# Expert weights loaded as halves of one matrix in 16 KB runs, and x1 stored in natural order, partly from ACT's queue

## The chip, the cores and the metric

The kernel runs on one core of one Trainium2 chip. The metric is the device time of one execution in microseconds. The kernel before took 1311.16 us, the median of three runs (1309.23 to 1311.32). Engines are named as in the profile: PE is TensorE (PEld its weight loads), DVE is VectorE, ACT is ScalarE, POOL is GpSimd, SP is SyncE, which here issues nearly all loads and stores. A name with a q behind it (SPq) is that engine's sequencer.

## What is computed

One decoder layer on 512 tokens of 1024 features, all in float32. A mixer (a causal convolution group and a dilated attention group) gives z = alpha * x + mix, and a layer norm of z gives x1. A router picks 4 of 32 experts for each token, and each expert is a SwiGLU block:

```python
g = jnp.minimum(xb @ w_gate[e] + b_gate[e], 7.0)
u = jnp.clip(xb @ w_up[e] + b_up[e], -7.0, 7.0)
hdn = (u + 1.0) * g * jax.nn.sigmoid(1.702 * g)
y = hdn @ w_down[e] + b_down[e]
```

The gated sum of the chosen experts' y is added to alpha * x1, and a second layer norm gives the output. Each expert has three matrices of 1024 x 1024 float32, 4 MB each, so 12 MB per expert and 403 MB in all, and every weight is read once.

## The kernel before, in words

**Front (0 to about 270 us).** The mixer, the first layer norm, the router and the ranks of tokens within their experts. The order of this part is made by a planner (class Plan): each operation is entered with its engine, an estimated duration, what it reads and writes, and a group; a list scheduler places the operations by rank (the longest chain behind an operation, less a tuned offset for its group, LAGS), and every engine's program, and the order in which DMAs are issued, follows the planned order. DMAs are one planned resource, D, and all of them are issued by SP (`dma`, line 409). At its end, x1 of each of the four token tiles is made in `acc` (lines 911 to 923: scale on ACT, times g, plus b, each in two halves on DVE or POOL) and stored to the DRAM scratch `x1d` (line 926), one 512 KB store per tile. The features of a token stand in `acc` in a permuted order: 1024 = 8 blocks of 4 quarters of 32 columns, with quarter outermost. So a row of `x1d` (4 rows of 256 per token) is one quarter. ACT's later work at that place is a copy for the last router logits, a table load, and the exp of the gates (line 1255).

**Experts (about 270 to 1260 us).** Experts are taken in an order by size: each expert has room for 32, 64, 96 or 128 tokens, that is 1 to 4 "rows" (78 rows in all: five experts of four rows, eight of three, fifteen of two, four of one). A row is 32 tokens, whose four quarters stand on the four groups of 32 partitions. Four rows make a group, 20 in all. `gather` (line 1008) fetches the rows of a group from `x1d` by indirect DMAs from POOL, `xpose` (line 1049) transposes 32 x 32 blocks on DVE, so that features stand on partitions; both run ahead of the expert that needs them (LOOK = 2: rows are gathered during an expert, and transposed, at the earliest, at the end of the next).

`expert` (line 1066) runs one expert in six steps, one per weight piece of 2 MB. There are seven places for pieces in SBUF (six `wt`, one `wb`); `advance` (line 319) issues the loads of later pieces as places come free. A gate/up piece (line 297) holds 256 input rows of both matrices, so it takes two loads; a down piece (line 306) holds 512 rows of w_down. A partition gets single matrix rows, 4 KB in one run:

```python
SP.dma_start(t[:, :, gu], src[0, ei, c * 256:(c + 1) * 256, :].rearrange("e (k p) f -> p (e k) f", p=128))
```

In the steps c = 0 to 3 each row of the expert runs 2 x 4 matmuls of 32 stationary columns and 512 moving ones (gate and up side by side, one per quarter of the outputs; line 1078). A float32 matmul is two records in the trace, so a row has 64 records of 107 ns each in this phase, spread over four column groups of TensorE. Gate and up of a row share one PSUM bank (`ps[i]`: 2 x 256). After c = 3 `swiglu` (line 1055) runs five operations per row on DVE (clamp of gate, clamp of up, two products, and the transpose into `hT`, line 1064) and one on ACT. Then two down pieces follow (lines 1104 and 1107): two neighbouring rows share matmuls of 512 columns, a single row takes 256. The result is copied as a high and a low part (lines 1121 and 1123), and `combine` (line 1125) later adds a group's results to `acc` by one-hot matmuls (lines 1135 and 1136), two pairs at a time between the steps (`tick`, `fill`).

**End.** The bias sum (line 1320), the second layer norm of the four tiles (`outputs`, line 1414), the last expert's row (`last_rows`, line 1449), and a scatter of 32 rows. The norm's g and b are read through views that undo the permuted order.

Of the kernel before, what the change touches and what calls it, by code (L numbers as in the profile page):

```python
# [14 lines left out]
AF = mybir.ActivationFunctionType  # L15
# [249 lines left out]
def tile_layer(ctx: ExitStack, tc: tile.TileContext, x, positions, w_in, conv_w, conv_b, conv_ln_g,  # L265
# [143 lines left out]
    def dma(nbytes, dst, src, r=(), w=(), **kw):  # L409
        return op("D", max(0.45, nbytes / 359e3), lambda e: SP.dma_start(dst() if callable(dst) else dst, src), r, w, **kw)  # L410
# [465 lines left out]
    stores = []  # L876
# [4 lines left out]
    for tt in range(TT):  # L881
# [12 lines left out]
        def choose(e, lst=lst, lg=lg, tt=tt):  # L894
# [17 lines left out]
        zv, gv, bv = ((lambda f=f: f().rearrange("p (b q c) -> p q b c", b=8, q=4)) for f in (  # L912
            lambda zn=zn: zn.t(), lnps[0], lnps[1]))
        az = acc[:, tt].rearrange("p (q b c) -> p q b c", b=8, q=4)
# [3 lines left out]
        for hf in range(2):  # L918
            bs = slice(hf * 4, hf * 4 + 4)
            op("VG", (0.6, 1.25), (lambda az, zv, gv, bs: lambda e: (V if e == "V" else G).tensor_tensor(  # L920
                az[:, :, bs], zv()[:, :, bs], gv()[:, :, bs], OP.mult))(az, zv, gv, bs),
               [zn, ("ln", 0)], [("z", tt, 0), ("z", tt, 1), ("x1", tt, hf)])
            op("VG", (0.6, 1.25), (lambda az, bv, bs: lambda e: (V if e == "V" else G).tensor_tensor(
                az[:, :, bs], az[:, :, bs], bv()[:, :, bs], OP.add))(az, bv, bs), [("ln", 1)], [("x1", tt, hf)])
        stores.append(("x1d", tt))
        dma(524288, x1d[tt * 512:(tt + 1) * 512, :].rearrange("(p q) c -> p (q c)", q=4), acc[:, tt], r=[("x1", tt, hf) for hf in range(2)], w=[("x1d", tt)])
# [122 lines left out]
    def xpose(st, rows=None):  # L1049
# [3 lines left out]
        V.transpose(st["xT"][:, n].rearrange("p r b t -> p (r b t)"), st["xg"][:, n].rearrange("p r c -> p (r c)"))  # L1053
# [506 lines left out]
```

## Time and profile before

| | |
|---|---|
| median of three runs | 1311.16 us |
| the profiled execution | 1312.21 us |
| its span in the trace | 1310.2 us |
| mean granted clock of TensorE | 0.977 of full speed |
| PE / PEld / DVE / ACT / POOL busy | 1231.8 / 562.2 / 649.0 / 280.7 / 185.6 us |
| DMA moved | 441.95 MB, of it 436 MB read from DRAM |

Busy time of TensorE is not TensorE at its peak: matmuls are pipelined, four of them run side by side here, and their ends are modelled. Pace is better read from the starts of two groups in a timeline and the number of records between them. Idle time of an engine matters only where something on the path to the end waits for it. [...]

### The profile page before, as it was taken

The numbers are of one execution on the slowest core, as the hardware profiler recorded it, in microseconds if no ns is written. First come the engines' busy times: TensorE is split into PE (matmuls) and PEld (weight loads), VectorE is DVE, ScalarE is ACT, GpSimd is POOL, SyncE is SP. The second block draws the span as 40 slices with busy tenths as digits, with TensorE's granted clock in tenths as the row PEclk, the third lists the DMA queues.
The fourth block names the chain that finished last, engine by engine and source line by source line (L and its number), as shares of the span: only waits on it lengthen the run. The fifth ranks groups of instructions, "written<-read, shape, count | busy, mean of one in ns | idle before, by whom it ended". The sixth has DMA issues, their size and how long they took to land. (4 is left out here: it accounts for less than half of the span.)

```text
span 1310.2 us, 25490 instructions
## 1 busy us (share of the span) xinstructions
PE 1231.8 (94%) x10578; PEld 562.2 (43%) x10578; DVE 649.0 (50%) x1516; ACT 280.7 (21%) x551; POOL 185.6 (14%) x158
## 2 busy tenths in 40 slices
PE   8989999889998999999999999998999998999984
PEld 7867767723232333332333323343345333534342
DVE  5999855745442443343424434353425462444474
ACT  4677782311000000000000001110111110111122
POOL 2854101321011011011010110011100101000003
PEclk9999999889999999999999999999999999999987
DMA  9400335679999999999999999999999999999991
GB/s 286 165 1 1 129 113 141 241 287 389 408 406 406 408 406 406 409 396 406 409 406 408 406 406 405 409 405 408 405 408 408 405 406 406 391 364 356 409 401 71
DMA packets 126003, 441.95 MB, mean 337 GB/s; under 512 B 8279, under 2 KB 16615, under 8 KB 125884
## 3 DMA queue, kind: packets, MB, share of 16 engines
q1 hardware_dynamic: 122092, 429.98, 84.4%
q0 software_dynamic: 3792, 10.29, 2.2%
q8 instruction: 85, 1.39, 0.4%
q14 instruction: 34, 0.28, 0.1%
HBM read 435.99 MB, written 4.33 MB: 336 GB/s over the span
## 5 line engine op out<-in xcount | busy, mean ns | idle before, releaser
L1078 PE MATMUL gd<-wt,xTg 128*32 128x512 f32 x4304 | 494.9, 596 | 9.9 <-DMA wt<-in_exp_w_up_dram 4.9
L1078 PEld LDWEIGHTS gd<-wt,xTg 128*32 128x32 f32 x4304 | 146.3, 110 | 287.4 <-issue 273.8
L1104 PE MATMUL gd<-wt,hT 128*32 128x512 f32 x1472 | 184.7, 594 | 16.2 <-DVE hT L1064 13.2
L1017 POOL DMA_INDIRECT xg<-x1d,idx x78 | 74.7, 957 | 879.5 <-DVE tk L1046 837.0
L1137 DVE TENSOR_TENSOR acc<-acc,cb 128x512 f32<-128x512 f32 x160 | 102.4, 678 | 167.5 <-PE cb L1136 167.4
L1060 ACT ACTIVATE sg<-gm 128x256 f32<-128x256 f32 x78 | 32.5, 417 | 594.9 <-DVE gm L1059 594.9
L1123 DVE TENSOR_TENSOR yl<-gd,wh 32x256 fp32r<-32x256 f32 (+1 forms) x140 | 73.8, 527 | 141.7 <-ACT wh L1121 140.4
L1121 ACT ACTIVATE wh<-gd 32x256 fp32r<-32x256 f32 (+1 forms) x140 | 64.7, 462 | 280.0 <-PE gd L1104 201.3
L1104 PEld LDWEIGHTS gd<-wt,hT 128*32 128x32 f32 x1472 | 54.9, 110 | 126.9 <-issue 83.9
L1059 DVE TENSOR_SCALAR gm<-gd 128x256 f32<-128x256 f32 x77 | 30.9, 401 | 107.9 <-PE gd L1078 107.9
L546 PE MATMUL bk<-wt,wh 128*128 128x512 f32 (+1 forms) x352 | 80.9, 377 | 0.7 <-ACT sg L590 0.7
L1078 PE MATMUL gd<-wb,xTg 128*32 128x512 f32 x624 | 73.5, 593 | 1.3 <-DMA wb<-in_exp_w_up_dram 1.3
L1135 PE MATMUL cb<-wh,cg 128*128 128x512 f32 (+2 forms) x160 | 72.4, 453 | 2.2 <-DVE cg L1129 2.2
L1107 PE MATMUL gd<-wt,hT 128*32 128x256 f32 x1056 | 68.0, 387 | 6.2 <-DMA wt<-in_exp_w_down_dram 4.9
L584 DVE SCALAR_TENSOR_TENSOR bk<-u,cT,bk 128x512 f32<-128x512 f32 x88 | 66.2, 753 | 1.9
L546 PEld LDWEIGHTS bk<-wt,wh 128*128 128x128 f32 x352 | 61.2, 189 | 13.3 <-ACT sg L590 1.1
L1136 PE MATMUL cb<-yl,cg 128*128 128x512 f32 (+2 forms) x160 | 64.4, 402 | 0.0
L1135 PEld LDWEIGHTS cb<-wh,cg 128*128 128x128 f32 (+2 forms) x160 | 30.8, 192 | 57.9 <-issue 40.4
L1107 PEld LDWEIGHTS gd<-wt,hT 128*32 128x32 f32 x1056 | 41.3, 111 | 31.8 <-issue 11.7
L1063 DVE SCALAR_TENSOR_TENSOR um<-um,tk,sg 128x256 f32<-128x256 f32 x78 | 39.7, 509 | 8.9
L546 PE MATMUL bk<-wt,wl 128*128 128x512 f32 (+1 forms) x176 | 41.5, 378 | 1.6 <-DVE wl L537 1.6
L582 POOL TENSOR_TENSOR cv<-cv,acc 128x512 f32<-128x512 f32 x28 | 40.1, 1435 | 8.2 <-ACT acc L579 6.7
(336 smaller groups left out, 1210.3 us busy)
## 6 DMA issues: line engine op xcount, KB each, us to landing
wt<-in_exp_w_gate_dram SPq DMA_DIRECT2D x112, 1024.0 KB, 19.7
wt<-in_exp_w_up_dram SPq DMA_DIRECT2D x112, 1024.0 KB, 18.9
wt<-in_exp_w_down_dram SPq DMA_DIRECT2D x52, 2048.0 KB, 20.4
wb<-in_exp_w_down_dram SPq DMA_DIRECT2D x12, 2048.0 KB, 17.1
wb<-in_exp_w_gate_dram SPq DMA_DIRECT2D x16, 1024.0 KB, 18.4
wb<-in_exp_w_up_dram SPq DMA_DIRECT2D x16, 1024.0 KB, 19.5
wt<-in_w_in_dram SPq DMA_DIRECT2D x3, 2048.0 KB, 13.1
acc<-in_x_dram SPq DMA_DIRECT2D x8, 512.0 KB, 8.0
```

What stands on the lines that cost most here:

```text
L546: P.matmul(b.t[:, ts], w.t[:, k], xx[:, k, ts], start=(pas == 0 and k == 0), stop=(pas == 2 and k == KT - 1))
L582: op("G", 1.25, (lambda t: lambda e: G.tensor_tensor(cv[:, c], cv[:, c], t.t, OP.add))(t), [t], [k])
L584: op("V", 0.663, (lambda j: lambda e: V.scalar_tensor_tensor(b.t, u[:, c, j:j + T], cT[:, c, j:j + 1], b.t, op0=OP.mult, op1=OP.add))(j), ...
L1017: G.indirect_dma_start(out=xg[:, r], out_offset=None, in_=x1d[:, :], in_offset=bass.IndirectOffsetOnAxis(ap=idx[:, r:r + 1], axis=0))
L1078: P.matmul(ps[i][q * 32:(q + 1) * 32], st["xT"][:, r, c * 2 + k], w[:, k, :, :, q], start=False, stop=(c == 3 and k == 1))
L1104: P.matmul(d[j * 32:(j + 1) * 32], st["hT"][:, r + j % 2, c * 4 + k], w[:, k, 2 * (j // 2):2 * (j // 2) + 2], **kw)
L1107: P.matmul(d[j * 32:(j + 1) * 32, 0:256], st["hT"][:, r, c * 4 + k], w[:, k, j], **kw)
L1121: S.activation(st["yh"][o], a, AF.Copy)
L1123: V.tensor_tensor(st["yl"][o], a, st["yh"][o].bitcast(F32), OP.subtract)
L1135: P.matmul(ps, cg[0:n, tt * 128:(tt + 1) * 128], st["yh"][0:n, c], start=True, stop=False)
L1136: P.matmul(ps, cg[0:n, tt * 128:(tt + 1) * 128], st["yl"][0:n, c], start=False, stop=True)
L1137: V.tensor_tensor(acc[:, tt, c], acc[:, tt, c], ps, OP.add)
```

## The change

1. Loads. An expert's six pieces are halves (512 input rows) of one matrix: gate half 0, up half 0, gate half 1, up half 1, then the two halves of down. Partition p gets four consecutive matrix rows, 4p to 4p + 3, which is 16 KB in one run in DRAM and in SBUF. Each piece is one load.
2. Since a partition now holds features 4p to 4p + 3 of a half, `xpose` and `swiglu` hand the DVE transposes a view of their input that takes every fourth column: block k of a half takes columns k, k + 4, k + 8 and so on.
3. Each gate/up matmul covers one matrix: 256 moving columns instead of 512, four k-blocks per piece instead of two. Outputs, biases, norms and the down projection go by features in natural order; the quarter views with blocks of 32 are gone.
4. x1 is made in natural order. Its store becomes two per tile, one per half, with runs of 128 floats (512 bytes), and the stores of tiles 2 and 3 are issued from ACT's queue. The planner still books them on D.

```diff
-        def gu_piece(c):
-            def f():
-                ei = e()
-                t = piece().rearrange("p (k g) f -> p k g f", g=2)
-                for gu, src in enumerate((exp_w_gate, exp_w_up)):
-                    SP.dma_start(t[:, :, gu], src[0, ei, c * 256:(c + 1) * 256, :].rearrange("e (k p) f -> p (e k) f", p=128))
-                got[tag, "gu", c] = t
-            return f
-
-        def dn_piece(c):
+        def half(src, kind, c, h):
+
             def f():
                 ei = e()
                 t = piece()
-                SP.dma_start(t, exp_w_down[0, ei, c * 512:(c + 1) * 512, :].rearrange(
-                    "e (k p) f -> p (e k) f", p=128))
-                got[tag, "dn", c] = t
+                SP.dma_start(t.rearrange("p k f -> p (k f)"),
+                             src[0, ei, h * 512:(h + 1) * 512, :].rearrange("e (p k) f -> p (e k f)", k=4))
+                got[tag, kind, c] = t
             return f

-        return [gu_piece(c) for c in range(4)] + [dn_piece(c) for c in range(2)]
+        return [half((exp_w_gate, exp_w_up)[c % 2], "gu", c, c // 2) for c in range(4)] + [
+            half(exp_w_down, "dn", h, h) for h in range(2)]
...
-    def dma(nbytes, dst, src, r=(), w=(), **kw):
-        return op("D", max(0.45, nbytes / 359e3), lambda e: SP.dma_start(dst() if callable(dst) else dst, src), r, w, **kw)
+    def dma(nbytes, dst, src, r=(), w=(), q=SP, **kw):
+        return op("D", max(0.45, nbytes / 359e3), lambda e: q.dma_start(dst() if callable(dst) else dst, src), r, w, **kw)
...
-            bs = slice(hf * 4, hf * 4 + 4)
+            bs = slice(hf * 512, hf * 512 + 512)
...
-        stores.append(("x1d", tt))
-        dma(524288, x1d[tt * 512:(tt + 1) * 512, :].rearrange("(p q) c -> p (q c)", q=4), acc[:, tt], r=[("x1", tt, hf) for hf in range(2)], w=[("x1d", tt)])
+        stores.extend(("x1d", tt, hf) for hf in range(2))
+        for hf in range(2):
+            dma(262144, x1d[tt * 512:(tt + 1) * 512, hf * 128:(hf + 1) * 128].rearrange("(p q) j -> p q j", q=4),
+                acc[:, tt, hf * 512:(hf + 1) * 512].rearrange("p (q j) -> p q j", q=4), r=[("x1", tt, hf)],
+                w=[("x1d", tt, hf)], q=S if tt > 1 else SP)
...
-        V.transpose(st["xT"][:, n].rearrange("p r b t -> p (r b t)"), st["xg"][:, n].rearrange("p r c -> p (r c)"))
+        V.transpose(st["xT"][:, n].rearrange("p r b t -> p (r b t)"),
+                    st["xg"][:, n].rearrange("p r (h c k) -> p (r h) k c", h=2, k=4))
...
-        V.transpose(st["hT"][:, r].rearrange("p b t -> p (b t)"), um)
+
+        V.transpose(st["hT"][:, r].rearrange("p b t -> p (b t)"), um.rearrange("p (h c k) -> p h k c", h=2, k=4))
...
-            w = got[tag, "gu", c].rearrange("p k g (b q c) -> p k g b q c", b=8, q=4)
+            h, g = divmod(c, 2)
+            w = got[tag, "gu", c].rearrange("p k (h q j) -> p k q h j", h=2, q=4)
...
-                for k in range(2):
+                for k in range(4):
                     for q in range(4):
-                        P.matmul(ps[i][q * 32:(q + 1) * 32], st["xT"][:, r, c * 2 + k], w[:, k, :, :, q], start=False,
-                                 stop=(c == 3 and k == 1))
+                        P.matmul(ps[i][q * 32:(q + 1) * 32, g], st["xT"][:, r, h * 4 + k], w[:, k, q], start=False,
+                                 stop=(c == 3 and k == 3))
...
-            w = got[tag, "dn", c].rearrange("p k (b q c) -> p k q b c", b=8, q=4)
+            w = got[tag, "dn", c]
...
-                                     w[:, k, 2 * (j // 2):2 * (j // 2) + 2], **kw)
+                                     w[:, k, j // 2 * 512:j // 2 * 512 + 512], **kw)
...
-                V.tensor_tensor(o.rearrange("p (b q c) -> p q b c", b=8, q=4),
-                                zn[tt - 1].rearrange("p (q b c) -> p q b c", q=4, b=8), gv, OP.mult)
+                V.tensor_tensor(o, zn[tt - 1], g2, OP.mult)
```

## Rows read from the trace of the kernel before

**Rows 1.** Windows: us, busy us of PE, PEld, DVE, ACT, POOL; PEclk, DMA share, GB/s.
```profile
400.00:500.00 100.00, 94.85 (x852) 30.92 (x848) 38.22 (x88) 8.07 (x16) 7.27 (x8) 1.00 1.03 407
895.00:905.00 10.00, 7.56 (x68) 2.75 (x63) 2.37 (x9) 1.50 (x4) 0.00 (x0) 0.83 1.02 408
1150.00:1200.00 50.00, 50.00 (x461) 19.15 (x457) 25.00 (x51) 5.19 (x12) 0.00 (x0) 1.00 1.00 374
```

**Rows 2.** The DMA view: all packets, then issues (count, size, median us to landing).
```profile
DMA packets 126003, 441.95 MB, mean 337 GB/s; under 512 B 8279, under 2 KB 16615, under 8 KB 125884
...
wt<-in_exp_w_down_dram SPq DMA_DIRECT2D x52, 2048.0 KB, 20.4
...
xg<-x1d,idx POOLq DMA_INDIRECT x78, 5.8
```

**Rows 3.** Waits of TensorE: us in total, times, longest us.
```profile
PE gd L1104 <- DVE hT L1064: 13.2, 16, 1.1
...
PE gd L1107 <- DMA wt<-in_exp_w_down_dram: 4.9, 4, 1.9
PE gd L1078 <- DMA wt<-in_exp_w_up_dram: 4.9, 3, 2.4
...
PE gd L1107 <- issue: 2.7, 2, 1.3
...
PE gd L1078 <- DMA wb<-in_exp_w_up_dram: 1.3, 1, 1.3
```

**Rows 4.** Timeline of TensorE, 894 to 904 us: start, us, instructions [idle before <-releaser].
```profile
898.05 3.47 PE L1078 MATMUL gd<-wt,xTg 128*32 128x512 f32 x16 [2.44 <-DMA wt<-in_exp_w_up_dram]
901.22 0.67 PE L1075 MATMUL gd<-wl,selr 96*32 96x512 bf16 x4
```

**Rows 5.** Timeline of TensorE, 1076 to 1092 us.
```profile
1085.85 3.55 PE L1107 MATMUL gd<-wt,hT 128*32 128x256 f32 x32 [1.95 <-DMA wt<-in_exp_w_down_dram]
1089.15 0.54 PE L1075 MATMUL gd<-wl,selr 96*32 96x512 bf16 x4
```

**Rows 6.** Timeline of TensorE, 900 to 925 us.
```profile
910.92 10.51 PE L1078 MATMUL gd<-wt,xTg 128*32 128x512 f32 x96
921.25 1.02 PE L1104 MATMUL gd<-wt,hT 128*32 128x512 f32 x2
```

**Rows 7.** Timeline of TensorE, 1226 to 1240 us.
```profile
1228.69 3.66 PE L1107 MATMUL gd<-wt,hT 128*32 128x256 f32 x64
1232.28 1.98 PE L1320 MATMUL cb<-wt,cg 32*128 32x512 f32 x4
```

**Rows 8.** Windows again, with w_in loads in 2 KB runs.
```profile
34.00:36.00 2.00, 2.00 (x11) 1.65 (x10) 1.97 (x3) 1.98 (x4) 2.00 (x2) 1.00 1.05 388
```

**Rows 9.** Groups of VectorE by form: count, busy us, mean ns of one, idle before.
```profile
L1064 DVE STREAM_TRANSPOSE hT<-um 128x256 f32<-128x256 f32 x78 | 34.7, 445 | 2.7
...
L1053 DVE STREAM_TRANSPOSE xTg<-xg 128x1024 f32<-128x1024 f32 x18 | 21.9, 1219 | 1.9 <-DMA xg<-x1d,idx 1.9
...
L1288 DVE CAST aux<-cb 128x384 bf16<-128x384 f32 x1 | 1.2, 1234 | 0.0
...
L1261 DVE TENSOR_REDUCE Gf<-hT 128x128 f32<-128x512 f32 x1 | 1.1, 1079 | 0.0
```

**Rows 10.** Timeline of all engines, 404 to 409 us.
```profile
404.12 0.43 DVE L1059 TENSOR_SCALAR gm<-gd 128x256 f32<-128x256 f32 x1 [4.61 <-PE gd L1078]
...
408.64 0.64 PE L1104 MATMUL gd<-wt,hT 128*32 128x512 f32 x4 [1.11 <-DVE hT L1064]
```

**Rows 11.** Timeline of all engines, 258 to 275 us.
```profile
263.42 0.32 SPq L410 DMA_DIRECT2D x1d<-acc  x1
...
269.38 0.22 ACT L1255 ACTIVATE key<-key 128x16 f32<-128x16 f32 x1 [8.57 <-DVE key L1254]
...
273.59 0.45 DVE L1053 STREAM_TRANSPOSE xTg<-xg 128x256 f32<-128x256 f32 x1 [1.27 <-DMA xg<-x1d,idx]
```

**Rows 12.** Waits of TensorE again, for VectorE's reading of the logits.
```profile
PE bk L872 <- DVE sel L899: 1.1, 1, 1.1
```

More of the change, by code (lines that the diff above doesn't have):

```diff
@@ L911, in tile_layer @@
         zn = buf("zn")
-        zv, gv, bv = ((lambda f=f: f().rearrange("p (b q c) -> p q b c", b=8, q=4)) for f in (
-            lambda zn=zn: zn.t(), lnps[0], lnps[1]))
-        az = acc[:, tt].rearrange("p (q b c) -> p q b c", b=8, q=4)
+        zv, gv, bv = (lambda zn=zn: zn.t()), lnps[0], lnps[1]
+        az = acc[:, tt]
         op("A", 1.13, (lambda tt, lst, zn: lambda e: S.activation(
@@ L918, in tile_layer @@
         for hf in range(2):
[L919 removed]
+            bs = slice(hf * 512, hf * 512 + 512)
             op("VG", (0.6, 1.25), (lambda az, zv, gv, bs: lambda e: (V if e == "V" else G).tensor_tensor(
[L921 removed]
+                az[:, bs], zv()[:, bs], gv()[:, bs], OP.mult))(az, zv, gv, bs),
                [zn, ("ln", 0)], [("z", tt, 0), ("z", tt, 1), ("x1", tt, hf)])
             op("VG", (0.6, 1.25), (lambda az, bv, bs: lambda e: (V if e == "V" else G).tensor_tensor(
[L924 to L926 removed]
+                az[:, bs], az[:, bs], bv()[:, bs], OP.add))(az, bv, bs), [("ln", 1)], [("x1", tt, hf)])
+        stores.extend(("x1d", tt, hf) for hf in range(2))
[3 more added lines that the diff above has]
+                w=[("x1d", tt, hf)], q=S if tt > 1 else SP)
     pl.group = "rank0"
@@ L1074, in expert @@
                     for q in range(4):
-                        P.matmul(ps[i][q * 32:(q + 1) * 32], sel[0:96], bv[:, :, :, q], start=True, stop=False)
-                for k in range(2):
+                        P.matmul(ps[i][q * 32:(q + 1) * 32], sel[0:96], bv[:, q], start=True, stop=False)
+                for k in range(4):
                     for q in range(4):
-                        P.matmul(ps[i][q * 32:(q + 1) * 32], st["xT"][:, r, c * 2 + k], w[:, k, :, :, q], start=False,
-                                 stop=(c == 3 and k == 1))
+                        P.matmul(ps[i][q * 32:(q + 1) * 32, g], st["xT"][:, r, h * 4 + k], w[:, k, q], start=False,
+                                 stop=(c == 3 and k == 3))
                 if c:
@@ L1104, in expert @@
                             P.matmul(d[j * 32:(j + 1) * 32], st["hT"][:, r + j % 2, c * 4 + k],
-                                     w[:, k, 2 * (j // 2):2 * (j // 2) + 2], **kw)
+                                     w[:, k, j // 2 * 512:j // 2 * 512 + 512], **kw)
                         else:
-                            P.matmul(d[j * 32:(j + 1) * 32, 0:256], st["hT"][:, r, c * 4 + k], w[:, k, j], **kw)
+                            P.matmul(d[j * 32:(j + 1) * 32, 0:256], st["hT"][:, r, c * 4 + k],
+                                     w[:, k, j * 256:(j + 1) * 256], **kw)
             advance()
@@ L1314, in add_bias @@
         V.tensor_copy(GT[0:NE], ps[0:NE])
-        bdp = t[0:NE, 0].rearrange("p (b q c) -> p q b c", b=8, q=4)
         yield
@@ L1319, in add_bias @@
                 ps = cb.tile([128, 512], F32, name="cb")
-                P.matmul(ps, GT[0:NE, tt * 128:(tt + 1) * 128], bdp[:, 2 * hf:2 * hf + 2], start=True, stop=True)
+                P.matmul(ps, GT[0:NE, tt * 128:(tt + 1) * 128], t[0:NE, 0, hf * 512:(hf + 1) * 512], start=True,
+                         stop=True)
                 c = slice(hf * 512, (hf + 1) * 512)
@@ L1441, in outputs @@
             qs = slice(q * 32, (q + 1) * 32)
-            S.activation(gl_[qs].rearrange("p (b c) -> p b c", b=8), quarter(got["last"][:, 0], q), AF.Copy)
+            S.activation(gl_[qs], quarter(got["last"][:, 0], q), AF.Copy)
         yield
     def quarter(t, q):
-        return t[q * 32:(q + 1) * 32].rearrange("p (b q c) -> p q b c", b=8, q=4)[:, q]
+        return t[q * 32:(q + 1) * 32, q * 256:(q + 1) * 256]
     def last_rows():
@@ L1462, in last_rows @@
             qs = slice(q * 32, (q + 1) * 32)
-            V.scalar_tensor_tensor(ol[0:32].rearrange("p (b q c) -> p q b c", b=8, q=4)[:, q],
-                                   zl[qs].rearrange("p (b c) -> p b c", b=8), st[qs, 14:15], quarter(got["last"][:, 1], q),
+            V.scalar_tensor_tensor(ol[0:32, q * 256:(q + 1) * 256], zl[qs], st[qs, 14:15], quarter(got["last"][:, 1], q),
                                    op0=OP.mult, op1=OP.add)
```

3 lines of the change are left out of this document (1 added, 2 removed).

## The prediction

> **What bounds the kernel now.** I read the stretches first. While the experts run the loads come at 407 GB/s with the DMA engines' share at full, and TensorE is busy 95% of the same time; late, from 1150 us, TensorE is busy without a gap while the rate falls to 374 GB/s [rows 1]. So two limits lie almost on each other: a 2 MB piece lands 20 us after its issue, of which its own transfer at 407 GB/s is 5 us, so about four pieces are always in flight, and yet TensorE seldom waits [rows 1, 2]. Which one ends last is read from TensorE's waits: over the whole run it waits 11.1 us for expert weights, in eight waits, and 13.2 us, in 16 waits, for the transposed hidden rows of its own expert (hT) [rows 3]. Nearly all the rest of its time between 274 and 1260 us is work. [...] On the other side, an expert of one row waits 1.3 us for its hT at the start of its down projection even where the weights are there (the two waits put down to "issue" [rows 3]), and one of the weight waits of that line stands at such an expert; I take 1.3 off. So faster weights can give back 11.1 - 1.3 + 3.0 = 13 us at most, and after that the end is set by TensorE's work and by VectorE's chain in front of the second half of each expert.
>
> **Part 1, the loads.** Per expert and partition, 24 runs of 4 KB become six of 16 KB (a piece is four rows in one run); bytes and pieces stay, and a gate/up piece needs one load in place of two, so SP issues 128 fewer; SP mostly waits for free pieces, so that is worth nothing. The packets are now 4 KB (of 126003, all but 119 are under 8 KB [rows 2]). What a longer run gives is not in the trace; the nearest rows are 2 KB runs, at 388 GB/s with the engines full, against 4 KB runs at 407 [rows 8, 1]. A packet of each of 16 engines thus takes 84.5 ns at 2 KB and 161.0 at 4 KB: 76.5 ns per 2 KB and 8 ns fixed. At 16 KB that is 620 ns, or 423 GB/s, 3.9% more. Lower end: nothing, if a run is cut into 4 KB packets all the same; upper end 428 GB/s, without a fixed part. I take 423. Over some 800 us to the last weight wait, shortly after 1089 [rows 5], that is 31 us of lead where 13 are needed (1.6%, 414 GB/s), so all of it comes back: **-13 us**; the rest shows as engines that are no longer full.
>
> Two things pay for long packets: row gathers of later experts, which land 5.8 us after issue [rows 2], share the engines. If each of a gather's eight descriptors per engine waits for one 16 KB packet in place of a 4 KB one, it lands 8 x 0.46 = 3.7 us later. That is hidden: rows are gathered one whole expert before they are transposed, 10 us at the shortest. Without that cover it would be 3.7 us for each of 20 groups.
>
> **Part 2, the matmuls.** A piece now holds one matrix, so each gate/up matmul of 512 columns becomes two of 256: 4992 more matmul records and as many weight loads. The price is in the trace, since single rows already run the down projection at 256 columns: 64 in 3.59 us, which is 64 x 53.8 ns and one change of shape of 0.15 [rows 7]; the wide ones take 107.6 each (96 in 10.33 us [rows 6]). Two narrow ones cost one wide one, and that run, which has a weight load for each matmul, shows the loads hidden. **0 us**; upper end 4992 x 2 x 56.1 - 4992 x 107.6 ns = 23 us, if the change of shape were paid in proportion; I take 0, because long runs show it once per run.
>
> **Part 3, the transposes.** With four features of a partition side by side, both VectorE transposes read every fourth float (16 bytes apart) where they read neighbours before. Today: 445 ns for 256 columns and 1219 for 1024, so 1.01 ns per element and 186 ns fixed [rows 9]. No row has a step of 16 bytes. The nearest are a reduction over steps of 128 bytes, (1079 - 186)/512 = 1.74 ns per element, and a copy from PSUM that writes with steps of 10 bytes, (1234 - 186)/384 = 2.73 [rows 9]. So 256 columns gain between 0 (nothing excludes it) and 0.44 us; I take the reduction's, the one that reads SBUF with steps: 0.73 x 256 = **0.19 us**.
>
> [...]
>
> Where it lands: hT's transpose is the last of five VectorE operations, and the rows of an expert queue on VectorE: two rows take from 404.12, the first clamp, to 408.64, when TensorE is let go, so 2.2 us each [rows 10]. Each of the 16 hT waits [rows 3] thus grows by two transposes, 16 x 2 x 0.19 = 6.1 us; four experts of one row grow by one each, 0.8 us: **+7 us**. The transposes of gathered rows (18 of 1024 columns, +0.75 us each) stand behind hT and ahead of the next PSUM copies while TensorE runs 3.4 us and more of down projection; I cost them at nothing, except the first, +0.2 us on the path at 273.59 [rows 11].
>
> Could the gate's clamp now start early, its sum being finished one piece sooner? Gate and up share a PSUM bank, and the trace shows a bank kept in order as a whole: TensorE's next router logits wait 1.1 us for VectorE's reading of other columns of that bank [rows 12]. So it waits for up's last matmul as before: 0.
>
> **Part 4, the stores of x1.** Each becomes two halves in runs of 512 bytes; those of tiles 2 and 3 go to ACT's queue. The last is issued at 263.42, as soon as its data is there; the first gathered rows are transposed at 273.59, after a wait for their landing [rows 11]. The last half is 256 KB: at the 388 GB/s of short runs [rows 8] it saves up to 0.65 us against 512 KB; at half that rate nothing. I take -0.2, which cancels the transpose's. On SP's queue only expert 0's last piece stands behind these stores; it could be issued earlier, and nobody needs it then. On ACT two pairs of stores wait; behind them stand a table load and the exp of 269.38, before which ACT is idle 8.57 us [rows 11], so 4 us of waiting cost nothing. If a store stood ahead of the copy for the last router logits it would cost some 4 us. Planned order and the chain of rank and slots, which is longer than that of stores, stay. The natural order of columns in down projection, norm and output changes access patterns but no count: 0.
>
> **Sum.** -13 + 7 + 0 = -6 us. The profiled execution took 1312.2 us (span 1310.2), 1.05 above the median of 1311.16; 1312.2 - 6 - 1.05 = 1305.
>
> **Rivals.**
> (a) The strided read is free: -13 us, 1298. For it: the transposes take about one float per ns and lane, with no sign that neighbours are read together [rows 9]. Against: the only reduction with steps is slow.
> (b) Packets stay at 4 KB, so the loads do not do what they say: the weights stay the limit to 1090 us, and TensorE's later hT disappears in fewer weight waits: 1311. Against: 119 packets of this trace are over 8 KB [rows 2].
> (c) Slower: the strided transposes cost more than the weights give. It decides at 13/36 = 0.36 us per transpose of 256 (805 ns in place of 445). At the copy's price that is 36 x 0.44 = 16 us, and the hT waits become as long as the weight wait behind which the clock fell [rows 4]; with two such falls, 1.5 us each, the sum is +6: 1317. For it: the copy [rows 9]; against: that one writes, and into 2-byte elements.
>
> **How the numbers follow.** Chances: forecast 0.42 (own range 1300 to 1310), (a) 0.25, (b) 0.13, (c) 0.20. About 0.2%, 2.6 us, can be told from no change, so faster is below 1308.5: three quarters of the forecast's cases, all of (a): 0.56. Slower, above 1313.8: most of (c) and a little of the rest: 0.20. The rest, (b) and edges, 0.24. The range reaches from below (a) to (c): 1295 to 1317.
>
> **What would show it.** Right: packets of 16 KB and a rate near 423 GB/s until pieces run ahead, then falling; weight waits of TensorE near 0; gate/up matmuls at 54 ns each; hT's transpose near 640 ns; hT waits 6 us longer in total; gathers landing at 8 to 10 us. Wrong: 445 ns (a), 407 GB/s and the same weight waits (b), 805 ns and more (c), new waits of TensorE on gathers, or a start of the experts later than 274 us.

## The result, and the profile after

The changed kernel took 1341.12 us, the median of four runs (1338.81 to 1342.25), against 1311.24 for the kernel before: a ratio of 1.0231, 95% interval 1.021 to 1.0252. One run of the kernel before, of 3457 us, is no part of the ratio. It is 30 us slower where 6 us faster was forecast. The profiled execution took 1342.25 us, its span 1340.2.

The page of the changed kernel first (engines and instructions, then the rate in 40 slices of the span, then packets):

```profile
PE 1258.9 (94%) x15570; PEld 727.3 (54%) x15570; DVE 682.3 (51%) x1516; ACT 280.7 (21%) x551; POOL 185.7 (14%) x158
...
GB/s 282 159 1 1 130 112 132 309 289 367 426 424 422 404 383 422 308 366 422 427 342 382 420 424 404 372 339 408 422 420 397 414 359 426 325 339 341 406 413 69
DMA packets 53911, 442.56 MB, mean 330 GB/s; under 512 B 6295, under 2 KB 18727, under 8 KB 29180
```

The loads do what they say: 53911 packets in place of 126003 [rows 2], and 420 to 427 GB/s in the undisturbed slices, where 423 was forecast and 407 was the rate before [rows 1]. What limits the rate in the other slices is no longer the loads. The waits of TensorE (in total, times, longest) answer to [rows 3]:

```profile
PE gd L1102 <- DVE hT L1061: 18.8, 17, 1.3
PE sl L1105 <- issue: 6.2, 1, 6.2
PE gd L1076 <- issue: 5.0, 11, 0.8
PE gd L1102 <- PE gd L1076: 4.8, 6, 0.9
PE gd L1105 <- issue: 4.6, 3, 1.5
```

No wait for weights is left, and hT's waits grew by 5.6 us, close to the forecast. One row is new: eleven waits of the gate/up matmuls (L1076 now) for "issue", that is, for nothing that the profile shows. Its 5.0 us are not its price. The timeline of one of them, all engines, answers to the stretch of [rows 10] (start, us, instructions, idle before):

```profile
404.16 3.66 PE L1076 MATMUL gd<-wt,xTg 128*32 128x256 f32 x64
...
405.17 0.95 POOL L1012 DMA_INDIRECT xg<-x1d,idx  x1 [24.69 <-DVE tk L1041]
406.42 0.95 POOL L1012 DMA_INDIRECT xg<-x1d,idx  x1 [0.30 <-issue]
...
407.63 2.85 PE L1076 MATMUL gd<-wb,xTg 128*32 128x256 f32 x20
407.68 0.95 POOL L1012 DMA_INDIRECT xg<-x1d,idx  x1 [0.30 <-issue]
407.94 0.24 PEld L1076 LDWEIGHTS gd<-wb,xTg 128*32 128x32 f32 x5 [0.18 <-issue]
408.67 0.14 PEld L1076 LDWEIGHTS gd<-wb,xTg 128*32 128x32 f32 x2 [0.48 <-issue]
408.93 0.95 POOL L1012 DMA_INDIRECT xg<-x1d,idx  x1 [0.30 <-issue]
409.38 0.18 PEld L1076 LDWEIGHTS gd<-wb,xTg 128*32 128x32 f32 x6 [0.58 <-issue]
410.81 1.27 PEld L1076 LDWEIGHTS gd<-wb,xTg 128*32 128x32 f32 x28 [1.25 <-issue]
410.82 1.53 PE L1076 MATMUL gd<-wb,xTg 128*32 128x256 f32 x24 [0.33 <-issue]
411.92 0.42 DVE L1055 TENSOR_SCALAR gm<-gd 128x256 f32<-128x256 f32 x1 [6.95 <-PE gd L1076]
```

The first 64 matmuls go at full pace (3.66 us with the tail of the last). Then the weight loads come in twos, fives and sixes, with pauses between, while POOL issues four row gathers one behind the other; 0.9 us after the fourth ends (408.93 + 0.95), TensorE runs on at full pace. The matmul row calls itself busy for 2.85 of these 3.2 us: busy time, and even the idle in brackets, hides a stop of this kind, and the weight loads show it. (The window ends at 412 us, so the last group is not shown whole.) All eleven stand at the gathers of a group.

Busy time being no measure here, I use VectorE's first operation of each row of an expert, the clamp of the gate (L1055; L1059 before): 77 of its 78 instances are recorded in each of the traces compared here, in the same order. How much longer or shorter the stretch between two neighbouring clamps became tells where time went. Summed from the first to the last of them (295.48 and 1250.33 us before, 297.49 and 1281.50 after) that gives, from one trace of each kernel (yl is the low part of an expert's result):

| us against before | until the first clamp | four intervals of the weight waits | interval of a wait for yl | intervals longer by over 0.85 us | the rest | at the last clamp |
|---|---|---|---|---|---|---|
| changed kernel | +2.0 | -6.2 | -2.5 | +26.2 (14 of them) | +11.6 | +31.2 |
| the same without indirect gathers (e13, below) | -3.5 | -12.9 | -0.8 | +3.9 (2) | +12.5 | -0.7 |
| before, narrow matmuls (e2) | +2.1 | -3.5 | -2.5 | +32.2 (14) | +2.6 | +31.0 |
| before, strided transposes (e7) | -0.8 | -12.8 | 0.0 | +10.4 (6) | +9.9 | +6.7 |
| before, 8 KB runs (e4) | +2.1 | -11.5 | -1.0 | +9.5 (7) | +1.0 | +0.1 |
| 8 KB runs, late gathers (e11) | -1.7 | -13.1 | -2.8 | +7.5 (4) | -0.1 | -10.2 |

The fourteen long intervals of the changed kernel are the loss, and twelve of them have a gather in them. The other two hold a fall of the granted clock behind a wait for hT, where the kernel before had none (window view: us, busy us of PE, PEld, DVE, ACT, POOL; PEclk, which is the granted clock of TensorE as a share of its full speed, DMA share, GB/s):

```profile
520.00:525.00 5.00, 4.17 (x24) 1.16 (x28) 2.69 (x3) 0.00 (x0) 0.00 (x0) 0.66 1.03 428
625.00:630.00 5.00, 3.71 (x21) 1.02 (x24) 3.43 (x4) 0.10 (x1) 0.00 (x0) 0.71 1.02 426
```

### The profile page after: what moved, and what is told of

The parts are those of the page before. It is cut to its first block, busy times and chain, and to the rows that moved or that the text cites. A ratio compares the mean times of both kernels' runs of the same rounds, so it can differ in the third digit from the quotient of the medians.

```text
span 1340.2 us, 34961 instructions
## 1 busy us (share of the span) xinstructions
PE 1258.9 (94%) x15570; PEld 727.3 (54%) x15570; DVE 682.3 (51%) x1516; ACT 280.7 (21%) x551; POOL 185.7 (14%) x158
## 2 busy tenths in 40 slices
DMA packets 53911, 442.56 MB, mean 330 GB/s; under 512 B 6295, under 2 KB 18727, under 8 KB 29180
## 3 DMA queue, kind: packets, MB, share of 16 engines
q0 software_dynamic: 3792, 10.29, 2.2%
## 5 line engine op out<-in xcount | busy, mean ns | idle before, releaser
L1076 PE MATMUL gd<-wt,xTg 128*32 128x256 f32 x8608 | 517.7, 380 | 6.6 <-issue 3.9
L1076 PEld LDWEIGHTS gd<-wt,xTg 128*32 128x32 f32 x8608 | 299.4, 110 | 198.1 <-issue 42.2
L1102 PE MATMUL gd<-wt,hT 128*32 128x512 f32 x1472 | 192.5, 604 | 22.8 <-DVE hT L1061 17.8
L1102 PEld LDWEIGHTS gd<-wt,hT 128*32 128x32 f32 x1472 | 52.5, 111 | 138.2 <-issue 88.6
L1055 DVE TENSOR_SCALAR gm<-gd 128x256 f32<-128x256 f32 x77 | 30.7, 399 | 121.8 <-PE gd L1076 116.5
L1076 PE MATMUL gd<-wb,xTg 128*32 128x256 f32 x1248 | 77.3, 380 | 1.4 <-issue 1.1
L1076 PEld LDWEIGHTS gd<-wb,xTg 128*32 128x32 f32 x1248 | 44.1, 110 | 29.2 <-issue 7.0
L1105 PEld LDWEIGHTS gd<-wt,hT 128*32 128x32 f32 x1056 | 38.0, 110 | 32.2 <-issue 10.5
L1061 DVE STREAM_TRANSPOSE hT<-um 128x256 f32<-128x256 f32 x78 | 50.6, 649 | 2.7
```

What stands on the lines that cost most here:

```text
L1061: V.transpose(st["hT"][:, r].rearrange("p b t -> p (b t)"), um.rearrange("p (h c k) -> p h k c", h=2, k=4))
L1076: P.matmul(ps[i][q * 32:(q + 1) * 32, g], st["xT"][:, r, h * 4 + k], w[:, k, q], start=False, stop=(c == 3 and k == 3))
L1102: P.matmul(d[j * 32:(j + 1) * 32], st["hT"][:, r + j % 2, c * 4 + k], w[:, k, j // 2 * 512:j // 2 * 512 + 512], **kw)
L1105: P.matmul(d[j * 32:(j + 1) * 32, 0:256], st["hT"][:, r, c * 4 + k], w[:, k, j * 256:(j + 1) * 256], **kw)
```

## The experiments

The first theory (G): narrow matmuls use instructions twice as fast, and beside a gather TensorE gets too few. Rivals: L, 16 KB packets keep TensorE's instruction packets waiting on the same DMA engines; N, twice the instructions cost at any time. (The 28 us of stops that the expectations name came from group starts and recorded matmuls, so missing records count as lost time in it; the clamps do not have that fault.) Each ratio is to the kernel before, run again beside that experiment; its median there was 1311.2 to 1314.4 us, so times of different experiments can differ by 0.25% for that alone.

**e1: short packets in the changed kernel.**

```diff
-                SP.dma_start(t.rearrange("p k f -> p (k f)"),
-                             src[0, ei, h * 512:(h + 1) * 512, :].rearrange("e (p k) f -> p (e k f)", k=4))
+                rows = src[0, ei, h * 512:(h + 1) * 512, :].rearrange("e (p k) f -> p (e k) f", k=4)
+                for k in range(4):
+                    SP.dma_start(t[:, k], rows[:, k])
```

> The changed kernel, with each piece fetched by four loads of one matrix row per partition, so packets of 4 KB; instructions of TensorE, the strided transposes and the stores stay as changed. Theory G (TensorE stops because matmuls of 256 columns use instructions twice as fast as before while POOL issues the row gathers; the length of the packets has no part in it): the stops of 1 to 4.5 us inside gate/up runs stay, 28 us in all, at the same eleven gathers, and the time is 1336 to 1346 us (TensorE, 30 us later than before, needs the weights later, so 407 GB/s hardly holds it up). Rival L (packets of 16 KB hold up TensorE's instruction packets on the same DMA engines): the stops are gone, 1341 - 28 = 1313 us, up to 11 us more for weight waits that come back, so 1311 to 1325.

Measured: 1358.25 us, ratio 1.0345 (1.0313 to 1.0377). The stops are still there and cost more: the long intervals hold 38.3 us in place of 26.2, and "issue" waits of the gate/up matmuls are 25 in place of eleven. Rival L falls: with short packets the stops cost more, not less. G's range was too low; whether the shorter packets or the four times as many loads make them worse, this run does not tell.

**e2: narrow matmuls in the kernel before.**

```diff
-                        P.matmul(ps[i][q * 32:(q + 1) * 32], st["xT"][:, r, c * 2 + k], w[:, k, :, :, q], start=False,
-                                 stop=(c == 3 and k == 1))
+                        for g in range(2):
+                            P.matmul(ps[i][q * 32:(q + 1) * 32, g], st["xT"][:, r, c * 2 + k], w[:, k, g, :, q],
+                                     start=False, stop=(c == 3 and k == 1 and g == 1))
```

> The kernel before, with each gate/up matmul of 512 columns issued as two of 256 (one for gate, one for up); loads in 4 KB runs, transposes and stores as before. Theory G: stops inside gate/up runs appear at the gathers, some 28 us, of which up to 11 us are given back by weight waits that TensorE no longer meets: 1325 to 1340 us. Rival L (long packets): no such stops, 1309 to 1314. Rival N (twice the instructions cost at all times, by a floor per instruction, not at the gathers): the time is also up, but the gate/up matmuls outside gathers take more than 53.8 ns each.

Measured: 1341.53 us, ratio 1.0228 (1.0197 to 1.026), just above theory G's range. Part 2 of the change alone costs 30 us, as much as the whole change. Its waits have the same new row:

```profile
PE gd L1105 <- DVE hT L1064: 13.5, 16, 1.1
PE gd L1079 <- issue: 6.2, 15, 0.6
```

Outside the gathers neighbouring clamps keep their distance (+2.6 us in 57 intervals), so rival N falls: a narrow matmul costs half a wide one, as forecast (64 narrow ones in 3.66 us with the tail of the last, at 404.16 above, against 96 wide ones in 10.33 [rows 6]).

**e3, e6: plain loads for the gathers.** `xg` is loaded from fixed rows, so the experts work on wrong rows; the rest of the changed kernel stays.

```diff
-            G.indirect_dma_start(out=xg[:, r], out_offset=None, in_=x1d[:, :],
-                                 in_offset=bass.IndirectOffsetOnAxis(ap=idx[:, r:r + 1], axis=0))
+            S.dma_start(xg[:, r], x1d[r * 128:(r + 1) * 128, :])
```

(S is ACT's queue, e3; in e6 it is G, POOL's.)

> The changed kernel, with the indirect row gathers on POOL replaced by plain loads of as many bytes from fixed rows of x1d, issued from ACT's queue; the experts so work on wrong rows. Theory G: with no gather on POOL there is no stop inside a gate/up run, and 28 us or a little more are gained: 1303 to 1314 us. Rivals L and N (packet length or instruction count alone): the stops stay, at the places where an instruction packet is late, and the time is 1335 to 1345.

> The changed kernel with the indirect gathers replaced by plain loads of fixed rows, still issued by POOL (the experts work on wrong rows). If anything that POOL issues holds up TensorE (its writing of descriptors): the stops stay, 1330 to 1345 us. If only the indirect form does: as with the plain loads from ACT's queue, 1300 to 1310.

Measured: 1303.10 us (0.9927, 0.9898 to 0.9955) from ACT's queue and 1308.61 us (0.9958, 0.9943 to 0.9973) from POOL's. No stop is left in either. But a plain load does not wait for the tokens' numbers: in both runs the loads went out earlier, beside the down projection or at the change of expert, so two things had changed. These runs show that the stops go with the gathers, not what of a gather makes them. POOL's writing of descriptors, which e6's expectation names, is an assumption that no trace shows; what the traces have is the time of POOL's DMA instructions, 0.95 us for a gather and 0.54 for a plain load.

**e13, e14, e15: plain loads in the gathers' place.** A small operation that reads the tokens' numbers stands in front of the loads on the same queue:

```diff
+        G.tensor_tensor(xg[:, 0, 0:used], tk[:, 4:4 + used], tk[:, 4:4 + used], OP.add)
         for r in range(used):
-            G.indirect_dma_start(out=xg[:, r], out_offset=None, in_=x1d[:, :],
-                                 in_offset=bass.IndirectOffsetOnAxis(ap=idx[:, r:r + 1], axis=0))
+            G.dma_start(xg[:, r], x1d[r * 128:(r + 1) * 128, :])
```

(e14: an ACT copy and ACT's queue. e15: as e13, each load in two halves of 128 columns.)

> The changed kernel with plain loads of fixed rows issued by POOL in place of the indirect gathers, now held to the gathers' place: POOL first adds two columns of the gathered tokens' numbers, which VectorE has just made, so the four loads go out during the second or third gate/up step as the gathers do. (In the two runs with plain loads so far, the loads went out earlier, beside the down projection, so they tell nothing of the form of the load.) If what POOL issues as such (by software, 0.5 us each here) holds up TensorE: stops of 1 us and more at the same experts, 1320 to 1345 us. If only the indirect form does, or its length of 0.95 us each: 1303 to 1314.

> The same with the four plain loads issued from ACT's queue, behind a small ACT copy of the same columns, so in the gathers' place too. If the 512 KB of short rows that land at that time hold up TensorE, whoever issues them: stops remain, 1320 to 1345 us. If the cause lies with POOL's issuing: no stops, 1303 to 1314, whatever the POOL run gives.

> The changed kernel with POOL's plain loads in the gathers' place, as before, but each cut into two half-rows, so that POOL issues eight loads of 0.54 us one behind the other, 4.3 us in all, nearly as long as the 4.7 us of four gathers (four plain loads took 2.1 us, and TensorE runs on for 2.3 to 2.9 us after a first gather, so they could have been too short to show anything). If the length of POOL's issuing decides: stops of 1 to 2 us at the experts with gathers, 1318 to 1340 us. If the indirect form does: no stops, 1304 to 1314.

Measured: e13 1308.37 us (0.9955, 0.994 to 0.997), e14 1312.17 us (0.9983, 0.997 to 0.9996), e15 1305.08 us (0.9957, 0.9942 to 0.9973). None has a stop inside a gate/up run: after 300 us no two neighbouring weight loads of such a run start over 0.5 us apart, where e2 has 19 such pauses, 17 us in all. The timeline of e13, at the expert that was shown above:

```profile
396.95 3.66 PE L1076 MATMUL gd<-wt,xTg 128*32 128x256 f32 x64
397.57 0.19 POOL L1011 TENSOR_TENSOR xg<-tk 128x4 f32<-128x4 f32 x1 [25.90 <-DVE tk L1007]
...
398.06 2.14 POOL L1013 DMA_DIRECT2D xg<-x1d  x4 [0.30 <-POOL xg L1011]
...
400.42 3.64 PE L1076 MATMUL gd<-wb,xTg 128*32 128x256 f32 x64
402.40 0.43 DVE L1055 TENSOR_SCALAR gm<-gd 128x256 f32<-128x256 f32 x1 [4.64 <-PE gd L1076]
```

64 matmuls in 3.6 us through and behind the loads, and the clamp 2.0 us after the last group's start, where it took 4.3 us with gathers (407.63 to 411.92). e15's eight loads keep POOL at it for nearly as long as four gathers do, and again both groups run at full pace:

```profile
397.75 3.66 PE L1078 MATMUL gd<-wt,xTg 128*32 128x256 f32 x64
398.86 4.24 POOL L1015 DMA_DIRECT2D xg<-x1d  x8 [0.29 <-POOL xg L1011]
401.23 3.64 PE L1078 MATMUL gd<-wb,xTg 128*32 128x256 f32 x64
```

The profile lists e13's loads on the same queue as the gathers (q0, "software_dynamic"), with the same 3792 packets and 10.29 MB. So neither the bytes that land at that time, nor POOL issuing them on that queue, nor for how long, stops TensorE: the indirect form does. What of it does (POOL's longer instruction, the reading of the indices, the scattered rows in DRAM) these runs do not separate. e14's own loss is elsewhere, 5.1 us once, at the first expert, where ACT's queue has other work in front of a sigmoid.

**e10, e12: the gathers two steps later**, beside the down projection, in the changed kernel and in the one before:

```diff
-            if c == 1:
+            if c == 3:
                 finish(new)
```

> The changed kernel with the gathers of a group issued two steps later, after an expert's last gate/up step in place of its second, so that they run beside the down projection, whose matmuls of 512 columns need half the instructions per time. Theory G: most of the stops inside gate/up runs are gone and 20 to 35 us of the changed kernel's 1341 are gained: 1306 to 1321. If TensorE's stops come with the gathers wherever they stand (or from something else at that time): 1335 to 1345, with stops in the down projection.

> The kernel before with the gathers two steps later, and nothing else. Theory G with the weights as the limit of the kernel before: its gathers hold up nothing that the weights would not hold up next, so 1309 to 1315 us. Rival: the later gathers gain by themselves: 1298 to 1306.

Measured: e10 1315.75 us (1.0027, 1.0004 to 1.005), so some 26 us of the loss (1.0231 less 1.0027) come back by moving the gathers and nothing else; e12 1311.93 us (0.9983, 0.9972 to 0.9994). The timeline of e10:

```profile
410.65 5.79 PE L1102 MATMUL gd<-wt,hT 128*32 128x512 f32 x52 [1.31 <-DVE tk L1006]
...
411.38 0.95 POOL L1012 DMA_INDIRECT xg<-x1d,idx  x1 [21.20 <-DVE tk L1041]
412.63 0.95 POOL L1012 DMA_INDIRECT xg<-x1d,idx  x1 [0.30 <-issue]
413.88 0.95 POOL L1012 DMA_INDIRECT xg<-x1d,idx  x1 [0.31 <-issue]
```

Matmuls of 512 columns run through the same gathers without a stop. But at three experts the moved gathers meet the down projection of a single row, which has 256 columns, and there the intervals grow by 5.5 us in all in e10, 6.1 in e12 and 5.8 in e11. In e12, whose matmuls, loads and transposes are those of the kernel before, two of the three look like this:

```profile
922.61 0.99 PEld L1107 LDWEIGHTS gd<-wt,hT 128*32 128x32 f32 x19 [0.30 <-issue]
...
925.83 0.95 POOL L1017 DMA_INDIRECT xg<-x1d,idx  x1 [0.30 <-issue]
926.33 0.14 PEld L1104 LDWEIGHTS gd<-wb,hT 128*32 128x32 f32 x3 [1.00 <-issue]
927.78 0.19 PEld L1104 LDWEIGHTS gd<-wb,hT 128*32 128x32 f32 x8 [1.31 <-issue]
...
1026.70 2.67 PE L1107 MATMUL gd<-wt,hT 128*32 128x256 f32 x33
1028.19 0.95 POOL L1017 DMA_INDIRECT xg<-x1d,idx  x1 [0.30 <-issue]
...
1030.15 1.76 PE L1107 MATMUL gd<-wt,hT 128*32 128x256 f32 x28 [0.78 <-issue]
```

Narrow matmuls of the down projection stop too (TensorE runs on 1.0 us after the fourth gather's end), and at 926 us wide ones stop, behind narrow ones beside the same gathers. So it is less the width than the number of matmuls that the stretch has to hold. An estimate from the changed kernel's stretch above: between the first gather and running on (405.17 to 410.82) TensorE took some 65 to 73 matmuls, where 105 of 256 columns or 52 of 512 fit at full pace; wide ones alone pass. e12 gains almost nothing: its weight waits are still 10.0 us, against 11.1 [rows 3], and the three experts cost 6.1, so it does not show whether the gathers of the kernel before hold anything up.

**e5: the kernel before with plain loads from ACT's queue** (wrong rows again; the edit is e3's).

> The kernel before, with the indirect gathers on POOL replaced by plain loads of as many bytes from fixed rows, issued from ACT's queue (the experts work on wrong rows). Theory G: with matmuls of 512 columns the gathers hold up nothing, so 1308 to 1313 us, and the 38 us that their removal gave in the changed kernel belong to its narrow matmuls alone. Rival: gathers hold TensorE up in the kernel before too, if less: 1298 to 1307.

Measured: 1321.40 us, ratio 1.0059 (1.0038 to 1.0081): slower, which neither theory said. Its waits of TensorE give the reason, as far as they go: the weights are late more often.

```profile
PE gd L1077 <- DMA wt<-in_exp_w_up_dram: 15.1, 9, 3.0
...
PE gd L1106 <- DMA wt<-in_exp_w_down_dram: 4.9, 3, 1.9
PE gd L1077 <- DMA wb<-in_exp_w_up_dram: 3.7, 3, 2.4
PE gd L1103 <- DMA wt<-in_exp_w_down_dram: 3.4, 3, 1.6
```

27 us of weight waits stand here against 11.1 [rows 3]. Why plain loads make the weights later than gathers do, I did not try, so this run settles nothing about the gathers.

**e7: the strided transposes alone**, in the kernel before (features meet other weights than they should):

```diff
-        V.transpose(st["hT"][:, r].rearrange("p b t -> p (b t)"), um)
+        V.transpose(st["hT"][:, r].rearrange("p b t -> p (b t)"), um.rearrange("p (h c k) -> p h k c", h=2, k=4))
```

(and `xpose` likewise, as in the change.)

> The kernel before, with the two VectorE transposes reading every fourth column as in the changed kernel (so that hidden and input features meet other weights than they should), and nothing else. By the prediction's Part 3, +7 us at the hT waits, less what the weight waits (11 us) shrink because TensorE comes later: 1312 to 1319 us, with hT waits of 18 to 19 us in place of 13.2. Rival: the strided transposes cost more than that, 0.2 us in each of the 78 rows (the clamps of two rows of one expert stand 0.2 us further apart in the changed kernel), 15 us: 1322 to 1327.

Measured: 1318.99 us, ratio 1.0056 (1.0035 to 1.0076), at the upper end of the first range; hT's waits are 16.4 us, not 18 to 19. But the time is a sum of gains and losses. By the table the intervals of the weight waits gave 12.8 us back though the loads stayed at 4 KB (a TensorE that comes later needs no faster weights), the short intervals, where the transposes show, took 9.9, and six long ones took 10.4. Four of these, with a gather each and 6.0 us, stand in e4 too, whose transposes turned out free, so they are not the price of a transpose; the other two hold falls of the clock (its mean in this trace is 0.972 of full speed, 0.977 before).

**e4, e9: 8 KB runs with wide matmuls.** A partition gets two consecutive rows of gate and two of up; e9 leaves the down pieces and hT as before.

```diff
-                    SP.dma_start(t[:, :, gu], src[0, ei, c * 256:(c + 1) * 256, :].rearrange("e (k p) f -> p (e k) f", p=128))
+                    SP.dma_start(t[:, gu].rearrange("p k f -> p (k f)"),
+                                 src[0, ei, c * 256:(c + 1) * 256, :].rearrange("e (p k) f -> p (e k f)", k=2))
...
-        V.transpose(st["hT"][:, r].rearrange("p b t -> p (b t)"), um)
+        V.transpose(st["hT"][:, r].rearrange("p b t -> p (b t)"), um.rearrange("p (b c k) -> p b k c", b=4, k=2))
```

> The kernel before with long runs but without the narrow matmuls: a gate/up piece is again 256 rows of both matrices in matmuls of 512 columns, but a partition gets two consecutive rows (2p, 2p + 1) of each, 8 KB in one run, and a down piece two times 8 KB; blocks of 64 in place of 32 in the permuted order; both transposes read every second float. Loads of 8 KB: 16384 / (8 + 8192 x 76.5 / 2048) ... by the working of Part 1, 417 GB/s, enough against the weight waits (13 us). If a step of 8 bytes costs the transposes as much as one of 16 bytes, the time is that of the kernel before with transposes at 16 bytes, 1319, or a few us less: 1312 to 1319. If it costs about half, 1304 to 1311. If it costs nothing: 1296 to 1302. No stops inside gate/up runs by any of these, since instructions are as before.

> As the 8 KB kernel, but for the gate/up pieces alone: down pieces stay at 4 KB runs and the hidden rows' transpose (hT) at neighbouring columns; the gathered rows' transpose reads every second float. If the price of the strided transposes lies in hT alone (the gathered rows' stand beside the down projection): 1311 less 11 to 13 us of weight waits and clock, 1297 to 1302. Rival: four long pieces of six give an average rate of only 414 GB/s, just what is needed, so some weight waits stay: 1302 to 1309.

Measured: e4 1310.55 us (0.9969, 0.9955 to 0.9983), e9 1309.94 us (0.9963, 0.9946 to 0.9979). The transposes of the changed kernel, of e7 and of e4, by form (count, busy us, mean ns), in that order:

```profile
L1061 DVE STREAM_TRANSPOSE hT<-um 128x256 f32<-128x256 f32 x78 | 50.6, 649 | 2.7
L1048 DVE STREAM_TRANSPOSE xTg<-xg 128x1024 f32<-128x1024 f32 x18 | 37.6, 2088 | 0.0
```

```profile
L1065 DVE STREAM_TRANSPOSE hT<-um 128x256 f32<-128x256 f32 x78 | 50.3, 645 | 2.7
```

```profile
L1066 DVE STREAM_TRANSPOSE hT<-um 128x256 f32<-128x256 f32 x78 | 34.8, 446 | 2.7
```

A step of 8 bytes is free (446 ns against 445 [rows 9]), one of 16 bytes costs 0.20 us per 256 columns. So e4 has no transposes against the 11.5 us that it gets back from the weights, and yet does not come to the 1296 to 1302 us of a free transpose. The table shows where the rest is: 5.7 us in four experts of two rows with a gather, 2.9 in two intervals with a fall of the clock (its mean in this trace is 0.971), 0.9 in the first expert, and 2.1 before the first clamp (my expectation for e11 put the first two kinds together as gathers). e9 misses both of its ranges, with no weight wait left, so its rival falls. It has the same four intervals with gathers, and this is the timeline of one:

```profile
499.17 7.07 PE L1080 MATMUL gd<-wt,xTg 128*32 128x512 f32 x64
...
503.93 0.94 POOL L1018 DMA_INDIRECT xg<-x1d,idx  x1 [0.30 <-issue]
...
506.03 0.42 DVE L1061 TENSOR_SCALAR gm<-gd 128x256 f32<-128x256 f32 x1 [6.05 <-PE gd L1080]
...
508.42 1.02 PE L1106 MATMUL gd<-wt,hT 128*32 128x512 f32 x2 [2.18 <-issue]
```

Here TensorE's records run at full pace, but the clamp of the first of two rows starts at 506.03, where that row's last matmul, three quarters through the 64, is due at 499.17 + 48 x 0.1076 = 504.3. It starts 1.2 us after the last gather's end, much as TensorE ran on 0.9 us after it above. The kernel before, with the same gathers and matmuls, has no such delay. Why is open.

**e11: 8 KB runs and late gathers together**, the version that these runs point to.

> The 8 KB kernel (1310.6 us: matmuls of 512 columns, free transposes, loads at 417 GB/s) with the gathers two steps later as well. Its trace shows 1.4 us lost at each of seven experts with a gather in their last gate/up steps, 10 us in all, and 2 us at the first. Theory G (gathers and gate/up matmuls should not meet, at 512 columns too once the weights no longer set the pace): 1298 to 1304 us. Rival: that loss has nothing to do with gathers, and the later gathers cost what they cost the changed kernel at three experts: 1308 to 1316.

Measured: 1300.73 us, ratio 0.9902 (0.9884 to 0.992), faster than both kernels. It is some 9 to 10 us faster than e4 (1310.6 to 1300.7), but the traces do not give all of that to the gathers' move. The four delayed clamps are gone (7.1 us between the two traces), and the three experts with single rows take 5.8 more. Most of the rest lies where the clock had fallen in e4 and has not in e11 (a mean of 0.971 against 0.982): 3.8 us before the first clamp, 1.1 of them an earlier start of the experts (PEclk 0.50 from 274.0 to 280.6 us in e4, 1.00 in e11), and 5.8 in three later intervals. That the move keeps the clock up is not shown. No weight wait is among its longest waits of TensorE:

```profile
PE gd L1106 <- DVE tk L1012: 8.0, 9, 1.1
PE gd L1106 <- DVE hT L1066: 7.1, 9, 1.3
PE gd L1109 <- issue: 6.9, 7, 1.3
```

## Why the prediction was wrong

**The step that failed** is Part 2, "The price is in the trace ... **0 us**; upper end ... 23 us, if the change of shape were paid in proportion". Made alone, this part costs 30 us (e2), in stops beside the gathers. The price per matmul was right: 64 narrow ones in 3.6 us where no gather is near, as in [rows 7]. What was missing is a term for the stretches in which POOL issues indirect gathers: there TensorE does not get through twice the matmuls in the same time. The row that the price came from is a run of the down projection at the end, with no gather near it. The prediction looked at the gathers only from the side of their landing (8.6 us against the 8 to 10 forecast, and hidden, as it said), not at what TensorE does while they are issued. (Its eight descriptors per engine were an estimate, 128 rows on 16 engines; the profile of the kernel before lists 3792 packets on q0 for 79 indirect DMAs, 48 each or three per engine.) It named "new waits of TensorE on gathers" as a sign that it was wrong, and meant waits for their data. Between the changed kernel and e13 lie 31.9 us at the last clamp, 5.5 of them before the first.

**Part 1 was right.** 16 KB packets, 420 to 427 GB/s, no weight waits; in e13 the intervals of the weight waits shrink by 12.9 us, against 11.1 - 1.3 + 3.0 = 13. The 3.0 us of that sum, and the 1.5 for each fall in rival (c), are what two falls of the clock cost in the trace before, each to 0.50 of full speed behind a weight wait (the window view again):

```profile
898.50:901.00 2.50, 2.50 (x16) 0.79 (x12) 0.24 (x1) 0.00 (x0) 0.00 (x0) 0.50 1.03 411
902.00:904.00 2.00, 2.00 (x24) 0.79 (x20) 0.00 (x0) 0.00 (x0) 0.00 (x0) 1.00 1.03 410
1086.00:1089.00 3.00, 3.00 (x32) 1.50 (x30) 0.07 (x1) 0.00 (x0) 0.00 (x0) 0.50 1.02 407
```

There 16 matmuls take 3.17 us (898.05 to 901.22 [rows 4]) and 32 narrow ones 3.30 (1085.85 to 1089.15 [rows 5]), and either group would take 1.72 at the pace of [rows 6, 7], so 3.0 us in all. But e7 gets 12.8 there with runs of 4 KB, so in the changed kernel the loads and the later TensorE share that gain; what long runs give by themselves e11 shows best, 13.1 us with free transposes and a TensorE that comes to them 4 us and more earlier than before. The 119 long packets held against rival (b) told nothing of the loads: they are the instruction packets of the kernel before (85 on q8 and 34 on q14).

**Part 3 had the right price and the wrong count.** 0.204 us per transpose (649 less 445) against 0.19, and 0.87 against 0.75 for 1024 columns. So a step of 16 bytes is not free in these traces, where one of 8 is (446 ns, e4), and rival (a) falls with that. But the prediction laid the price only on 16 recorded waits and four single rows, 7 us. The clamps show it in nearly every row, since the rows of an expert queue on VectorE: 11.6 us in the short intervals of the changed kernel and 12.5 in those of e13, where 7 were counted. The two falls of the clock (PEclk 0.66 and 0.71 over five microseconds in the changed kernel), 3.9 us more, were not foreseen (a third in e13, at 407.7 us, takes 1.7 in the interval of the wait for yl); that the longer hT waits bring them is not shown, since e4 has two with free transposes. Rival (c) comes nearest: the transposes take nearly all that the weights give, but at the forecast's own price per transpose, not at 0.36 us.

**Part 4 was right** as far as it shows: the experts' first matmul starts at 274.43 us against 274.09. In the other traces with the changed front it starts between 271.3 and 274.2 us (276.9 in e1), so a few tenths could not be seen.

With the indirect gathers out of the way the whole change is faster than the kernel before, by 0.45% or 6 us (e13), which is the sum that was forecast. That is luck: its transposes were 5 us too cheap, and in e13's trace the stretch from the first clamp to the last is 2.8 us longer than before. The first clamp comes 3.5 us early, which no step of the sum held: the experts start 2.1 us earlier, and the clock does not fall as they start (PEclk 1.00 from 271.3 to 275.0 us, 0.52 from 273.5 to 277.0 in the kernel before).

## What to carry to other kernels

Here a matmul cut into halves cost the same per column in a clean stretch (53.8 ns for 256 columns, 107.6 for 512 [rows 7, 6]), but 30 us in all beside the gathers (e2); price such a cut in the stretch where indirect gathers are issued, and keep the gathers beside wide matmuls alone (that gave some 26 of the 30 us back, e10). For long DMA runs, two consecutive rows a partition (8 KB, 414 to 421 GB/s in the undisturbed slices of e4, a step of 8 bytes in the transposes, 446 ns against 445) gave what was needed and cost the transposes nothing. An operation that the rows of an expert queue for costs its price once per row, not once per recorded wait (0.20 us more per transpose, 11.6 us in the short intervals of the changed kernel where 7 were counted).

## What the runs showed of the hardware

Four indirect gathers from POOL, 0.95 us each and 1.25 us apart, stop TensorE again and again from about 2.5 us after the first (2.8 in the changed kernel at 405.17) until 0.9 to 1.0 us after the last, at 256 columns per matmul, in the gate/up steps (changed kernel, e2) and in the down projection of single rows (e12); matmuls of 512 columns pass (52 in 5.79 us at 410.65 in e10), except behind narrow ones beside the same gathers (pauses of 1.0 and 1.3 us at 926 us in e12); plain loads from POOL (0.54 us each, as many bytes, even eight in a row) or from ACT do not. Outside the gathers 64 matmuls of 256 columns with a weight load each take 3.6 us, so there the number of instructions costs nothing that shows. Whether it is the reading of instructions that fails beside a gather, no run here shows: the profile gives these stops no releaser, and the instruction packets that I take for TensorE's (q8, 16 KB each: 85 before and 124 in the changed kernel, 64 bytes for each of the 9984 further records of TensorE) take hardly longer beside the gathers of the changed kernel, 1.07 us in the median of the 13 that overlap a group of gathers, than elsewhere, 1.02 us. Nor do the runs show why the kernel with 8 KB runs and wide matmuls gets its first clamp late at some gathers and the kernel before does not.
